# Feed-forward transposes by a trip through HBM and 32x32 block turns on VectorE, in place of TensorE transposes

## The chip, the cores and the metric

One core of a Trainium2 chip. The core has TensorE (PE in the rows; PEld is its weight load), VectorE (DVE), ScalarE (ACT), GpSimd (POOL) and SyncE (SP), each with its own instruction stream, and 16 DMA engines that all queues share. DMAs are issued here by SP and by ACT, each in the order of its own stream. The metric is the device time of one execution in microseconds, median of the runs.

## The reference

One layer of a hybrid decoder trunk, 256 tokens by 2048 features, all in float32. Four token mixers run on one normalised input, their gated sum goes through `w_out`, and a feed-forward part with a short convolution over time follows. The change touches only that last part:

```python
h2 = rmsnorm(x, norm2_g)
u = causal_dwconv(h2 @ ffn_up, ffn_dw, ffn_db)   # 3 taps over time, per feature
a, v = jnp.split(u, 2, axis=-1)                  # 5632 features each
return x + (jax.nn.silu(a) * v) @ ffn_down
```

## The kernel before

**Products.** Every large product (`product`, L192) has 256 tokens, in two halves of 128 rows of PSUM, by 512 output features. The weights stream in from HBM: SP loads 1 MB (four slices of 128 input features by 512) into one of three `wr` buffers (L180). A *unit* is two of those slices. ACT copies a unit into a float32r tile `wh` (L187), DVE computes the rest `wl = wr - wh` (L189), and PE multiplies both with the stationary activations: eight matmuls with `wh` (L205 and L206), then four with `wl` (L211). `wh` and `wl` have three buffers each. At the end of each unit `step` (L148) takes one piece of waiting work from the list `later`.

**Feed-forward.** The 11264 features of `ffn_up` are done in 22 *halves* of 512: for each of 11 *pairs* one half of `a` and one of `v`. A half is one product of 8 units. `half` (L897) then moves the two accumulators to SBUF with the row scale (`pu`, L901, ACT). The product leaves tokens on the partitions, while the convolution and the next product want features there. So `conv` has PE transpose eight 128x128 blocks against the identity into PSUM (`pt`, L908). Each of the four feature blocks then gets its first tap and bias on ACT (L912), two shifted taps on DVE (L916) and, for `a`, the silu on ACT (L921). This is put on `later` and runs two units into the next product. `glu` (L933 and `split_out`) multiplies `a` and `v` and splits the result into `ah` and `al`, the stationary operand of the down product.

**Down products.** `DOWN = (3, 3, 2, 3)` says how many pairs one `down` call (L940) takes. A call runs four products (one per 512 output features) of two units a pair, and adds each to `x2` on DVE (L948). A group's `down` is issued after the first pair of the next group; the last group's also stores the result (L950, SP). Partition p of an activation tile's block j holds feature 128 j + p, and the rows of `ffn_down` are loaded in that order.

**Order.** The program is straight-line code. The tile framework orders each engine's stream from dependencies and code order; the copies of the next units stand ahead of the evacuation `pu` in ACT's stream, as far as the three `wh` buffers go.

Of the kernel before, what the change touches and what calls it, by code (L numbers as in the profile page):

```python
# [9 lines left out]
F32 = mybir.dt.float32  # L10
F32R = mybir.dt.float32r
U8 = mybir.dt.uint8
AF = mybir.ActivationFunctionType
ALU = mybir.AluOpType
# [3 lines left out]
P = 128  # L18
S = 256
NT = 2  # L20
D = 2048
KT = D // P
BW = 512
NB = 4
DFF = 5632
NPAIR = DFF // BW
# [11 lines left out]
NEG = -1e30  # L38
LOAD = 4 * BW
WR = 3  # L40
DOWN = (3, 3, 2, 3)
WINDOWS = (2, 4, 8, 16)


# [54 lines left out]
def layer(ctx, tc, a):  # L99
    nc = tc.nc  # L100
    V, A, T = nc.vector, nc.scalar, nc.tensor
# [4 lines left out]
    ffn_up = a["ffn_up"][0]  # L106
# [3 lines left out]
    ident = cst.tile([P, P], F32, name="ident")  # L110
# [11 lines left out]
    tpp = ctx.enter_context(tc.tile_pool(name="tpp", bufs=2, space=PSUM))  # L122
# [13 lines left out]
    def pump(ns):  # L136
        credit[0] += ns
        while bg and credit[0] > 0:
            try:
                credit[0] -= next(bg[0])  # L140
            except StopIteration:
                bg.pop(0)
        if not bg:
            credit[0] = 0.0

    later = []

    def step(ns):  # L148
        if later:
            f = later.pop(0)  # L150
            if f is not None:
                f()
        else:
            pump(ns)
# [13 lines left out]
    def wtile(name, dt, ks, n, size, bufs=None):  # L168
        w = wp.tile([P, size], dt, name=name, bufs=bufs)
        return w[:, : ks * BW].rearrange("p (j n) -> p j n", j=ks)[:, :, :n]  # L170

    def units(src, c0, n, sizes, loads):

        k0 = have = 0
        loads = list(loads)
        for ks in sizes:
            if k0 == have:
                m = loads.pop(0)
                raw = wtile("wr", F32, m, n, LOAD, WR)
                nc.sync.dma_start(  # L180
                    out=raw,
                    in_=src[k0 * P : (k0 + m) * P, c0 : c0 + n].rearrange("(j p) n -> p j n", p=P),
                )
                base, have = k0, k0 + m
            part = raw[:, k0 - base : k0 - base + ks]
            hi = wtile("wh", F32R, ks, n, 2 * BW)
            A.copy(out=hi, in_=part)  # L187
            lo = wtile("wl", F32R, ks, n, 2 * BW)
            V.tensor_tensor(out=lo, in0=part, in1=hi.bitcast(F32), op=ALU.subtract)  # L189
            yield k0, hi, lo  # L190
            k0 += ks

    def product(src, c0, n, stat, sizes=None, loads=None, tail=False):

        nk = len(stat)
        acc = [accp.tile([P, 512], F32, name="acc") for _ in range(NT)]
        for k0, hi, lo in units(src, c0, n, sizes or [2] * (nk // 2), loads or [4] * (nk // 4)):
            ks = hi.shape[1]
            for ts in ((0,), (1,)) if tail and k0 + ks == nk else ((0, 1),):
                for j in range(ks):  # L200
                    xh, xl = stat[k0 + j]
                    for t in ts:
                        s = slice(t * P, (t + 1) * P)
                        o = acc[t][:, :n]
                        T.matmul(o, xh[:, s], hi[:, j], start=(k0 + j == 0), stop=False)  # L205
                        T.matmul(o, xl[:, s], hi[:, j], start=False, stop=False)  # L206
                for j in range(ks):
                    xh, _ = stat[k0 + j]
                    for t in ts:
                        s = slice(t * P, (t + 1) * P)  # L210
                        T.matmul(  # L211
                            acc[t][:, :n], xh[:, s], lo[:, j], start=False, stop=(k0 + j == nk - 1)
                        )
            step(1200.0)
        return acc

    def rsqrt(pool, ssq, n, scale, tag):

        v = pool.tile([P, n], F32, name=tag + "v", tag=tag + "v")
        V.tensor_scalar(v, ssq, scale, EPS, ALU.mult, ALU.add)  # L220
        r = pool.tile([P, n], F32, name=tag + "r", tag=tag + "r")
        A.activation(r, v, AF.Sqrt)
        V.reciprocal(out=r, in_=r)
        e = pool.tile([P, n], F32, name=tag + "e", tag=tag + "e")
        V.tensor_tensor(out=e, in0=v, in1=r, op=ALU.mult)
        V.tensor_tensor(out=e, in0=e, in1=r, op=ALU.mult)
        V.tensor_scalar(e, e, -0.5, 1.5, ALU.mult, ALU.add)
        V.tensor_tensor(out=r, in0=r, in1=e, op=ALU.mult)
        return r
# [36 lines left out]
    with ExitStack() as ph1:  # L266
# [46 lines left out]
        def vec(name, i=0):  # L313
            return vecT[:, VEC[name] + i : VEC[name] + i + 1]
# [438 lines left out]
        with tc.tile_pool(name="pDB", bufs=1) as pp:  # L753
# [7 lines left out]
            acc = product(w_in, C_CZ + BW, BW, hS, sizes=(1, 1) + (2,) * 7, loads=(1, 1) + (2,) * 7)  # L761
# [13 lines left out]
            for t in range(NT):  # L775
                V.scalar_tensor_tensor(
                    out=sg[:, t], in0=acca[t], scalar=rstd[:, t : t + 1], in1=sg[:, t],
                    op0=ALU.mult, op1=ALU.mult,
# [6 lines left out]
            pw = pp.tile([P, 4, P], F32, name="pw")  # L785
# [47 lines left out]
        with tc.tile_pool(name="pA", bufs=1) as pp:  # L833
            za = pp.tile([P, NT, W_FOX], F32, name="za")
            fb = pp.tile([P, 8], F32, name="fb")
# [30 lines left out]
    h2S = []  # L866
    ss2 = p2.tile([P, NT, 4], F32, name="ss2")
    for d in range(4):
        acc = product(w_out, d * BW, BW, yS)
# [3 lines left out]
        hi = hp.tile([P, 4, S], F32R, name="h2h", tag="h2h")  # L873
        lo = hp.tile([P, 4, S], F32R, name="h2l", tag="h2l")
        for b in range(2):
            pt = tpp.tile([P, 2, S], F32, name="pt")
            for i in range(2):
                c = 4 * d + 2 * b + i
                for t in range(NT):
                    T.transpose(pt[:, i, t * P : (t + 1) * P], x2[:, t, c * P : (c + 1) * P], ident)  # L880
            for i in range(2):
                c = 4 * d + 2 * b + i
# [9 lines left out]
    rstd2 = rsqrt(p2, s2, NT, 1.0 / D, "x2")  # L892


    up_ = ctx.enter_context(tc.tile_pool(name="fu", bufs=2))

    def half(pair, is_v, u):  # L897
        acc = product(ffn_up, (NPAIR if is_v else 0) * BW + pair * BW, BW, h2S)
        pu = up_.tile([P, NT, BW], F32, name="pu")
        for t in range(NT):  # L900
            A.activation(pu[:, t], acc[t], AF.Identity, scale=rstd2[:, t : t + 1])  # L901

        def conv(b):
            pt = tpp.tile([P, 2, S], F32, name="pt")
            for i in range(2):
                c = 2 * b + i
                for t in range(NT):
                    T.transpose(pt[:, i, t * P : (t + 1) * P], pu[:, t, c * P : (c + 1) * P], ident)  # L908
            for i in range(2):
                c = 2 * b + i  # L910
                ch = (NPAIR if is_v else 0) * 4 + pair * 4 + c
                A.activation(  # L912
                    u[:, c], pt[:, i], AF.Identity, bias=vec("fb", ch), scale=vec("fw", 2 * 88 + ch)
                )
                for sh, tap in ((1, 1), (2, 0)):
                    V.scalar_tensor_tensor(  # L916
                        out=u[:, c, sh:], in0=pt[:, i, : S - sh], scalar=vec("fw", tap * 88 + ch),
                        in1=u[:, c, sh:], op0=ALU.mult, op1=ALU.add,
                    )
                if not is_v:  # L920
                    A.activation(u[:, c], u[:, c], AF.Silu)  # L921

        later.extend([None, lambda: (conv(0), conv(1))])

    def pair_up(pair):
        ua = up_.tile([P, 4, S], F32, name="ua")
        uv = up_.tile([P, 4, S], F32, name="uv")
        hi, lo = act_tiles()
        half(pair, False, ua)
        half(pair, True, uv)  # L930

        def glu():
            V.tensor_tensor(out=uv, in0=ua, in1=uv, op=ALU.mult)  # L933
            split_out(hi, lo, uv)

        later.append(glu)
        return hi, lo

    out = a["out"][0].rearrange("(t p) d -> p t d", p=P)

    def down(pairs, tiles, last):
        st = stationary(tiles)
        w = ffn_down[pairs[0] * BW : (pairs[-1] + 1) * BW]
        for d in range(4):
            ds = slice(d * BW, (d + 1) * BW)
            acc = product(w, d * BW, BW, st, tail=last and d == 3)
            for t in range(NT):
                V.tensor_tensor(out=x2[:, t, ds], in0=acc[t], in1=x2[:, t, ds], op=ALU.add)  # L948
                if last:
                    nc.sync.dma_start(out=out[:, t, ds], in_=x2[:, t, ds])  # L950

    pending = None
    p0 = 0
    for size in DOWN:
        pairs = list(range(p0, p0 + size))
# [10 lines left out]
def feature_columns(inputs):  # L966

    cols = [inputs[n][0].reshape(-1, P) for n in ("norm2_g", "pool_scale", "gla_og", "conv_ln_g", "conv_ln_b", "conv_db")]
    cols += [np.tile(inputs[n][0], 2)[None] for n in ("fox_qg", "fox_kg")]
    cols += [inputs[n][0].reshape(-1, P) for n in ("conv_dw", "ffn_dw", "ffn_db")]  # L970
    return np.ascontiguousarray(np.concatenate(cols, axis=0).T)


# [26 lines left out]
```

## Time and profile before

| | |
|---|---|
| median of 3 runs (lowest to highest) | 1529.78 us (1529.42 to 1529.83) |
| the profiled execution's own time | 1529.93 us |
| its span, first to last instruction | 1528.1 us |
| PE busy | 1522.4 us, 100% of the span |
| DVE, ACT busy | 952.2 us (62%), 769.9 us (50%) |
| moved over HBM | 291.12 MB, mean 191 GB/s |
| chain that ended last | PE 99%, DMA 1% |

The chain that ended last is followed back from the last instruction: at every step to what released it. Busy time of PE overlaps (matmuls are pipelined), so the pitch of matmuls, start to start, tells more than the duration of one.

### The profile page before, as it was taken

To read this page: it belongs to the slowest core of one execution; us is meant where nothing else is said; L and a number is where in the kernel's file an instruction comes from. 1 tells how busy PE (TensorE), PEld (TensorE's weight loads), DVE (VectorE), ACT (ScalarE), POOL (GpSimd) and SP (SyncE) were. 2 spreads that over 40 slices of the span, in tenths; PEclk is the share of its full clock that TensorE was granted. 3 is DMA by queue.
4 is the path that set the end of the run, shared out by engine and by line. 5 is a ranking of instruction groups with operands and counts; after the bars stand their busy time and mean duration, and the time that the engine had idled before them with its cause. 6 is when DMAs were issued, how large, how long until landed. Compare 5 with 4: busy or idle time off the path is not lost.

```text
span 1528.1 us, 18387 instructions
## 1 busy us (share of the span) xinstructions
PE 1522.4 (100%) x7196; PEld 1278.0 (84%) x7196; DVE 952.2 (62%) x1220; ACT 769.9 (50%) x961; POOL 0.2 (0%) x4
## 2 busy tenths in 40 slices
PE   9999999999999999999999999999999999999998
PEld 8888899878998888888888888888888888888887
DVE  7799755657565566566555566655566546655664
ACT  6444466545455544444455555434555345535542
POOL 0000000000000000000000000000000000000000
PEclk9999999999999999999999999999999999999999
DMA  9656656545664566657555555555555555565563
GB/s 295 225 188 205 200 178 212 173 151 179 184 214 144 164 203 203 196 172 248 185 175 191 193 179 179 193 193 187 199 179 180 194 193 191 173 206 184 182 206 124
DMA packets 150665, 291.12 MB, mean 191 GB/s; under 512 B 5665, under 2 KB 20914, under 8 KB 150194
## 3 DMA queue, kind: packets, MB, share of 16 engines
q1 hardware_dynamic: 149680, 288.22, 57.4%
q10 hardware_dynamic: 898, 1.74, 0.4%
q8 instruction: 56, 0.92, 0.2%
q14 instruction: 31, 0.25, 0.1%
HBM read 287.83 MB, written 2.10 MB: 190 GB/s over the span
## 4 chain that ended last, share of the span: by engine, by line
PE 99%; DMA 1%; ACT 0%; issue 0%; DVE 0%; ACTq 0%
PE acc L205 32%; PE acc L206 31%; PE acc L211 31%; PE pt L908 1%; PE mx L547 1%; PE mx L739 0%; DMA wr<-in_w_in 0%; PE mx L698 0%; PE pt L880 0%; PE pt L255 0%; DMA n1g<-in_n1T 0%; ACT wh L187 0%; PE mx L731 0%; PE pt L338 0%; PE mx L515 0%
## 5 line engine op out<-in xcount | busy, mean ns | idle before, releaser
L189 DVE TENSOR_TENSOR wl<-wr,wh 128x1024 fp32r<-128x1024 f32 (+4 forms) x545 | 646.9, 1191 | 474.4 <-ACT wh L187 469.8
L187 ACT CAST wh<-wr 128x1024 fp32r<-128x1024 f32 (+4 forms) x545 | 558.9, 1026 | 673.1 <-PE acc L206 603.2
L205 PE MATMUL acc<-wh,ah 128*128 128x512 f32 (+3 forms) x1344 | 515.0, 383 | 0.5 <-ACT wh L187 0.5
L206 PE MATMUL acc<-wh,al 128*128 128x512 f32 (+3 forms) x1344 | 512.0, 381 | 0.0
L211 PE MATMUL acc<-wl,ah 128*128 128x512 f32 (+3 forms) x1344 | 347.4, 380 | 0.0
L205 PEld LDWEIGHTS acc<-wh,ah 128*128 128x128 f32 x1344 | 252.8, 188 | 45.9 <-ACT wh L187 2.1
L206 PEld LDWEIGHTS acc<-wh,al 128*128 128x128 f32 x1344 | 252.8, 188 | 42.8 <-issue 0.6
L211 PEld LDWEIGHTS acc<-wl,ah 128*128 128x128 f32 x1344 | 249.1, 188 | 43.9
L205 PE MATMUL acc<-wh,h2h 128*128 128x512 f32 x704 | 275.7, 392 | 0.0
L206 PE MATMUL acc<-wh,h2l 128*128 128x512 f32 x704 | 274.2, 389 | 0.0
L211 PE MATMUL acc<-wl,h2h 128*128 128x512 f32 x704 | 188.2, 389 | 0.0
L211 PEld LDWEIGHTS acc<-wl,h2h 128*128 128x128 f32 x704 | 132.1, 188 | 27.5
L205 PEld LDWEIGHTS acc<-wh,h2h 128*128 128x128 f32 x704 | 132.2, 188 | 27.0
L206 PEld LDWEIGHTS acc<-wh,h2l 128*128 128x128 f32 x704 | 132.2, 188 | 26.8
L428 DVE SCALAR_TENSOR_TENSOR cacc<-up,vecT,cacc 128x256 f32<-128x256 f32 x120 | 51.0, 484 | 0.0
L205 PE MATMUL acc<-wh,oh 128*128 128x512 f32 x128 | 49.8, 389 | 0.0
L206 PE MATMUL acc<-wh,ol 128*128 128x512 f32 x128 | 49.8, 389 | 0.0
L916 DVE SCALAR_TENSOR_TENSOR ua<-pt,vecT,ua 128x255 f32<-128x255 f32 (+1 forms) x88 | 38.3, 477 | 8.8 <-ACT ua L912 8.0
L916 DVE SCALAR_TENSOR_TENSOR uv<-pt,vecT,uv 128x255 f32<-128x255 f32 (+1 forms) x88 | 37.0, 476 | 2.7 <-ACT uv L912 2.7
L211 PE MATMUL acc<-wl,oh 128*128 128x512 f32 x128 | 35.7, 393 | 0.0
L948 DVE TENSOR_TENSOR x<-acc,x 128x512 f32<-128x512 f32 x32 | 20.7, 686 | 20.7 <-PE acc L211 20.7
L356 DVE SCALAR_TENSOR_TENSOR gt<-acc,rstd,gb 128x512 f32<-128x512 f32 x32 | 22.6, 748 | 13.7 <-PE acc L211 13.7
(229 smaller groups left out, 645.4 us busy)
## 6 DMA issues: line engine op xcount, KB each, us to landing
wr<-in_ffn_up SPq DMA_DIRECT2D x88, 1024.0 KB, 4.9
wr<-in_w_in SPq DMA_DIRECT2D x76, 1024.0 KB, 5.1
wr<-in_ffn_down SPq DMA_DIRECT2D x44, 1024.0 KB, 5.0
wr<-in_w_branch SPq DMA_DIRECT2D x16, 1024.0 KB, 5.0
wr<-in_w_out SPq DMA_DIRECT2D x16, 1024.0 KB, 4.9
wr<-in_w_in SPq DMA_DIRECT2D x16, 772.0 KB, 4.5
wr<-in_w_in SPq DMA_DIRECT2D x8, 696.0 KB, 4.2
gb<-in_gate_b SPq DMA_DIRECT2D x16, 256.0 KB, 3.4
```

The lines of the kernel that those rows point to most:

```text
L187: A.copy(out=hi, in_=part)
L189: V.tensor_tensor(out=lo, in0=part, in1=hi.bitcast(F32), op=ALU.subtract)
L205: T.matmul(o, xh[:, s], hi[:, j], start=(k0 + j == 0), stop=False)
L206: T.matmul(o, xl[:, s], hi[:, j], start=False, stop=False)
L211: T.matmul(acc[t][:, :n], xh[:, s], lo[:, j], start=False, stop=(k0 + j == nk - 1))
L356: V.scalar_tensor_tensor(out=g[:, t], in0=acc[t], scalar=rstd[:, t : t + 1], in1=bias, op0=ALU.mult, op1=ALU.add,)
L428: V.scalar_tensor_tensor(out=acc[:, c], in0=up[:, c, j : j + S], scalar=vec("cw", 4 * j + c), in1=acc[:, c], op0=ALU.mult, op1=ALU.add,)
L547: T.matmul(pss[h][:, q * P : (q + 1) * P], l_, r_, start=True, stop=True)
L908: T.transpose(pt[:, i, t * P : (t + 1) * P], pu[:, t, c * P : (c + 1) * P], ident)
L916: V.scalar_tensor_tensor(out=u[:, c, sh:], in0=pt[:, i, : S - sh], scalar=vec("fw", tap * 88 + ch), in1=u[:, c, sh:], op0=ALU.mult, op1=AL ...
L948: V.tensor_tensor(out=x2[:, t, ds], in0=acc[t], in1=x2[:, t, ds], op=ALU.add)
```

## The change

The eight PE transposes of a half go. In their place `half` does four things.

- ACT writes `pu` with its four feature quarters (128 features each) outermost, and stores quarter q with one DMA into rows 32 q to 32 q + 31 of a scratch tensor `mem` in HBM (128 KB a DMA, in runs of 1 KB). The four token quarters (32 partitions each) become blocks along a row of `mem`. Token quarters and feature quarters have changed places.
- `fetch`: ACT loads `mem` back as `pw` (512 KB, one 4 KB row a partition).
- `turn`: two DVE transposes turn the 32x32 blocks of `pw` into `zt`, features on partitions. Partition p of block j now holds feature 4 p + j of the half, so the columns of `ffn_dw` and `ffn_db` are reordered on their way in, and the rows of `ffn_down` are loaded as `(p j)`.
- `conv(c)`: taps, bias and silu as before, for one block at a time, reading `zt` in SBUF where it was `pt` in PSUM.

These pieces no longer go through `later`. `after(n, engine, f)` sets one due n units on, and ties its instructions behind the latest `wh` copy (ACT) or `wl` subtraction (DVE) of that unit: fetch at 6, turn at 9, the four convolutions at 10 to 13, `glu` at 14. `DOWN` becomes `(3, 3, 2, 2, 1)`: the last `down` takes one pair and follows the `down` of two pairs.

```diff
@@ -38,7 +38,7 @@
 NEG = -1e30
 LOAD = 4 * BW
 WR = 3
-DOWN = (3, 3, 2, 3)
+DOWN = (3, 3, 2, 2, 1)
 WINDOWS = (2, 4, 8, 16)
 
 
@@ -145,7 +145,20 @@
 
     later = []
 
+    due = []
+    steps = [0]
+    mark = {}
+
+    def after(n, engine, f):
+
+        due.append((steps[0] + n, engine, f))
+
     def step(ns):
+        steps[0] += 1
+        for x in [x for x in due if x[0] <= steps[0]]:
+            due.remove(x)
+            with tc.issue_after(mark[x[1]].ins):
+                x[2]()
         if later:
             f = later.pop(0)
             if f is not None:
@@ -169,7 +182,7 @@
         w = wp.tile([P, size], dt, name=name, bufs=bufs)
         return w[:, : ks * BW].rearrange("p (j n) -> p j n", j=ks)[:, :, :n]
 
-    def units(src, c0, n, sizes, loads):
+    def units(src, c0, n, sizes, loads, rows):
 
         k0 = have = 0
         loads = list(loads)
@@ -179,22 +192,22 @@
                 raw = wtile("wr", F32, m, n, LOAD, WR)
                 nc.sync.dma_start(
                     out=raw,
-                    in_=src[k0 * P : (k0 + m) * P, c0 : c0 + n].rearrange("(j p) n -> p j n", p=P),
+                    in_=src[k0 * P : (k0 + m) * P, c0 : c0 + n].rearrange(rows, p=P),
                 )
                 base, have = k0, k0 + m
             part = raw[:, k0 - base : k0 - base + ks]
             hi = wtile("wh", F32R, ks, n, 2 * BW)
-            A.copy(out=hi, in_=part)
+            mark["A"] = A.copy(out=hi, in_=part)
             lo = wtile("wl", F32R, ks, n, 2 * BW)
-            V.tensor_tensor(out=lo, in0=part, in1=hi.bitcast(F32), op=ALU.subtract)
+            mark["V"] = V.tensor_tensor(out=lo, in0=part, in1=hi.bitcast(F32), op=ALU.subtract)
             yield k0, hi, lo
             k0 += ks
 
-    def product(src, c0, n, stat, sizes=None, loads=None, tail=False):
+    def product(src, c0, n, stat, sizes=None, loads=None, tail=False, rows="(j p) n -> p j n"):
 
         nk = len(stat)
         acc = [accp.tile([P, 512], F32, name="acc") for _ in range(NT)]
-        for k0, hi, lo in units(src, c0, n, sizes or [2] * (nk // 2), loads or [4] * (nk // 4)):
+        for k0, hi, lo in units(src, c0, n, sizes or [2] * (nk // 2), loads or [4] * (nk // 4), rows):
             ks = hi.shape[1]
             for ts in ((0,), (1,)) if tail and k0 + ks == nk else ((0, 1),):
                 for j in range(ks):
@@ -893,34 +906,56 @@
 
 
     up_ = ctx.enter_context(tc.tile_pool(name="fu", bufs=2))
+    scr = ctx.enter_context(tc.tile_pool(name="scr", bufs=2, space=bass.MemoryType.DRAM))
 
     def half(pair, is_v, u):
-        acc = product(ffn_up, (NPAIR if is_v else 0) * BW + pair * BW, BW, h2S)
-        pu = up_.tile([P, NT, BW], F32, name="pu")
+
+        n = (NPAIR if is_v else 0) + pair
+        acc = product(ffn_up, n * BW, BW, h2S)
+
+        pu = up_.tile([P, 4, NT, P], F32, name="pu")
         for t in range(NT):
-            A.activation(pu[:, t], acc[t], AF.Identity, scale=rstd2[:, t : t + 1])
-
-        def conv(b):
-            pt = tpp.tile([P, 2, S], F32, name="pt")
-            for i in range(2):
-                c = 2 * b + i
-                for t in range(NT):
-                    T.transpose(pt[:, i, t * P : (t + 1) * P], pu[:, t, c * P : (c + 1) * P], ident)
-            for i in range(2):
-                c = 2 * b + i
-                ch = (NPAIR if is_v else 0) * 4 + pair * 4 + c
-                A.activation(
-                    u[:, c], pt[:, i], AF.Identity, bias=vec("fb", ch), scale=vec("fw", 2 * 88 + ch)
-                )
-                for sh, tap in ((1, 1), (2, 0)):
-                    V.scalar_tensor_tensor(
-                        out=u[:, c, sh:], in0=pt[:, i, : S - sh], scalar=vec("fw", tap * 88 + ch),
-                        in1=u[:, c, sh:], op0=ALU.mult, op1=ALU.add,
-                    )
-                if not is_v:
-                    A.activation(u[:, c], u[:, c], AF.Silu)
-
-        later.extend([None, lambda: (conv(0), conv(1))])
+            A.activation(
+                pu[:, :, t], acc[t].rearrange("p (q x) -> p q x", q=4), AF.Identity, scale=rstd2[:, t : t + 1]
+            )
+
+        mem = scr.tile([P, 4 * NT * P], F32, name="mem")
+        for q in range(4):
+            A.dma_start(
+                out=mem[32 * q : 32 * q + 32].rearrange("r (k c) -> k r c", k=4),
+                in_=pu[:, q].rearrange("p t x -> p (t x)"),
+            )
+        pw = up_.tile([P, 4, NT, P], F32, name="pw")
+
+        def fetch():
+            A.dma_start(out=pw.rearrange("p k t x -> p (k t x)"), in_=mem)
+
+        zt = up_.tile([P, 4, S], F32, name="zt", bufs=1)
+
+        def turn():
+            for t in range(NT):
+                V.transpose(
+                    out=zt[:, :, t * P : (t + 1) * P].rearrange("p j (k i) -> p j k i", k=4),
+                    in_=pw[:, :, t].rearrange("p k (i j) -> p j k i", j=4),
+                )
+
+        def conv(c):
+            ch = n * 4 + c
+            A.activation(
+                u[:, c], zt[:, c], AF.Identity, bias=vec("fb", ch), scale=vec("fw", 2 * 88 + ch)
+            )
+            for sh, tap in ((1, 1), (2, 0)):
+                V.scalar_tensor_tensor(
+                    out=u[:, c, sh:], in0=zt[:, c, : S - sh], scalar=vec("fw", tap * 88 + ch),
+                    in1=u[:, c, sh:], op0=ALU.mult, op1=ALU.add,
+                )
+            if not is_v:
+                A.activation(u[:, c], u[:, c], AF.Silu)
+
+        after(6, "A", fetch)
+        after(9, "V", turn)
+        for c in range(4):
+            after(10 + c, "V", lambda c=c: conv(c))
 
     def pair_up(pair):
         ua = up_.tile([P, 4, S], F32, name="ua")
@@ -933,7 +968,7 @@
             V.tensor_tensor(out=uv, in0=ua, in1=uv, op=ALU.mult)
             split_out(hi, lo, uv)
 
-        later.append(glu)
+        after(14, "V", glu)
         return hi, lo
 
     out = a["out"][0].rearrange("(t p) d -> p t d", p=P)
@@ -943,7 +978,7 @@
         w = ffn_down[pairs[0] * BW : (pairs[-1] + 1) * BW]
         for d in range(4):
             ds = slice(d * BW, (d + 1) * BW)
-            acc = product(w, d * BW, BW, st, tail=last and d == 3)
+            acc = product(w, d * BW, BW, st, tail=last and d == 3, rows="(p j) n -> p j n")
             for t in range(NT):
                 V.tensor_tensor(out=x2[:, t, ds], in0=acc[t], in1=x2[:, t, ds], op=ALU.add)
                 if last:
@@ -967,7 +1002,8 @@
 
     cols = [inputs[n][0].reshape(-1, P) for n in ("norm2_g", "pool_scale", "gla_og", "conv_ln_g", "conv_ln_b", "conv_db")]
     cols += [np.tile(inputs[n][0], 2)[None] for n in ("fox_qg", "fox_kg")]
-    cols += [inputs[n][0].reshape(-1, P) for n in ("conv_dw", "ffn_dw", "ffn_db")]
+    cols += [inputs["conv_dw"][0].reshape(-1, P)]
+    cols += [inputs[n][0].reshape(-1, P, 4).transpose(0, 2, 1).reshape(-1, P) for n in ("ffn_dw", "ffn_db")]
     return np.ascontiguousarray(np.concatenate(cols, axis=0).T)
 
 
```

**ACT's stream, around one `v` half and the `a` half behind it, before.** `wh` is the weight copy, `pu` the evacuation of a half, `uv`/`ua` the first tap, `ah` the split of the pair's result:

```order
L901 ACTIVATE pu<-acc,x2r 128x512 x2
L187 CAST wh<-wr 128x1024 x2
L912 ACTIVATE uv<-pt,vecT 128x256 x4
L187 CAST wh<-wr 128x1024 x2
L234 CAST ah<-uv 128x1024
L187 CAST wh<-wr 128x1024 x4
L901 ACTIVATE pu<-acc,x2r 128x512 x2
```

**The same place after the change:**

```order
L918 ACTIVATE pu<-acc,x2r 128x4x128 x2
L924 DMA mem<-pu 4x32x256 x4
L200 CAST wh<-wr 128x1024 x3
L931 DMA pw<-mem 128x1024
L200 CAST wh<-wr 128x1024
L247 CAST ah<-uv 128x1024
L200 CAST wh<-wr 128x1024 x3
L944 ACTIVATE ua<-zt,vecT 128x256 x4
L200 CAST wh<-wr 128x1024
L918 ACTIVATE pu<-acc,x2r 128x4x128 x2
L953 ACTIVATE ua<-ua 128x256
```

Five DMAs a half now stand in ACT's stream; the fetch stands behind three weight copies, and the first taps of a half now stand after four more copies, one copy ahead of the next half's evacuation.

**DVE's stream, around the end of one pair, before.** `wl` is the weight subtraction:

```order
L189 TENSOR_TENSOR wl<-wr,wh 128x1024 x8
L916 SCALAR_TENSOR_TENSOR uv<-pt,vecT,uv 128x255 x2
L916 SCALAR_TENSOR_TENSOR uv<-pt,vecT,uv 128x254 x2
L916 SCALAR_TENSOR_TENSOR uv<-pt,vecT,uv 128x255 x2
L916 SCALAR_TENSOR_TENSOR uv<-pt,vecT,uv 128x254 x2
L189 TENSOR_TENSOR wl<-wr,wh 128x1024
L933 TENSOR_TENSOR uv<-ua,uv 128x1024
L189 TENSOR_TENSOR wl<-wr,wh 128x1024
L235 TENSOR_TENSOR al<-uv,ah 128x1024
```

**The same half after it:**

```order
L937 STREAM_TRANSPOSE zt<-pw 128x4x128 x2
L202 TENSOR_TENSOR wl<-wr,wh 128x1024
L948 SCALAR_TENSOR_TENSOR uv<-zt,vecT,uv 128x255
L948 SCALAR_TENSOR_TENSOR uv<-zt,vecT,uv 128x254
L202 TENSOR_TENSOR wl<-wr,wh 128x1024
L948 SCALAR_TENSOR_TENSOR uv<-zt,vecT,uv 128x255
L948 SCALAR_TENSOR_TENSOR uv<-zt,vecT,uv 128x254
L202 TENSOR_TENSOR wl<-wr,wh 128x1024
L948 SCALAR_TENSOR_TENSOR uv<-zt,vecT,uv 128x255
L202 TENSOR_TENSOR wl<-wr,wh 128x1024
L948 SCALAR_TENSOR_TENSOR uv<-zt,vecT,uv 128x254
```

The taps, eight in a row before, are spread between the weight subtractions, and two block turns stand ahead of them.

## Rows read from the trace of the kernel before

**Rows 1.** The page, busy time of PE (share of span, instructions).

```profile
PE 1522.4 (100%) x7196; PEld 1278.0 (84%) x7196; DVE 952.2 (62%) x1220; ACT 769.9 (50%) x961; POOL 0.2 (0%) x4
```

**Rows 2.** Chain of waits, one half: start us, length us, engine, tile, line.

```profile
834.37 0.91 PE acc L211 x4
835.28 0.87 PE pt L908 x8
...
854.32 0.91 PE acc L211 x4
857.04 0.91 PE acc L211 x4
```

**Rows 3.** Groups by line: count, busy us, mean ns, idle before.

```profile
L908 PE MATMUL pt<-ident,pu 128*128 128x128 f32 x176 | 22.8, 272 | 0.0
```

**Rows 4.** Waits from 800 us to the end: us in total, times, longest.

```profile
ACT wh L187 <- PE acc L206: 287.5, 191, 1.7
...
PEld acc L205 <- ACT wh L187: 0.7, 1, 0.7
```

**Rows 5.** Busy time in one half: stretch, PE, PEld, DVE, ACT, POOL, clock, DMA share, GB/s.

```profile
834.37:857.04 22.67, 22.67 (x106) 18.85 (x105) 15.18 (x18) 12.47 (x15) 0.00 (x0) 1.00 0.56 186
```

**Rows 6.** Timeline of ACT behind one evacuation: start, length, idle before.

```profile
829.93 1.26 ACT L901 ACTIVATE pu<-acc,x2r 128x512 f32<-128x512 f32 x2
831.69 1.06 ACT L187 CAST wh<-wr 128x1024 fp32r<-128x1024 f32 x1 [0.50 <-PE acc L206]
834.41 1.05 ACT L187 CAST wh<-wr 128x1024 fp32r<-128x1024 f32 x1 [1.66 <-PE acc L206]
```

**Rows 7.** DMA issues by line on ACT's and SP's sequencers: ns min/median/max.

```profile
L806 ACTq DMA_DIRECT2D gx<-in_consts x1: 335/335/335, 202.0 to 202.0; - x1
L813 ACTq DMA_DIRECT2D wab<-in_gla_ba x1: 532/532/532, 202.8 to 202.8; - x1
L180 SPq DMA_DIRECT2D wr<-in_ffn_down x44: 367/368/390, 947.4 to 1501.1; - x44
```

**Rows 8.** DMA queues (packets, MB, share of 16 engines); issues (KB, us to landing).

```profile
q1 hardware_dynamic: 149680, 288.22, 57.4%
q10 hardware_dynamic: 898, 1.74, 0.4%
...
wr<-in_ffn_down SPq DMA_DIRECT2D x44, 1024.0 KB, 5.0
...
out<-x SPq DMA_DIRECT2D x8, 256.0 KB, 2.4
...
sst<-in_consts ACTq DMA_DIRECT2D x1, 512.0 KB, 5.1
...
wab<-in_gla_ba ACTq DMA_DIRECT2D x1, 1.0 KB
```

**Rows 9.** Groups by line from 800 us on, or of the whole run (last row).

```profile
L187 ACT CAST wh<-wr 128x1024 fp32r<-128x1024 f32 x256 | 269.7, 1054 | 313.9 <-PE acc L206 287.5 <-issue 16.4 <-ACT wh L187 10.0
...
L901 ACT ACTIVATE pu<-acc,x2r 128x512 f32<-128x512 f32 x44 | 27.8, 682 | 0.0
L912 ACT ACTIVATE ua<-pt,vecT 128x256 f32<-128x256 f32 x44 | 23.4, 557 | 3.3 <-PE pt L908 3.3
...
L948 DVE TENSOR_TENSOR x<-acc,x 128x512 f32<-128x512 f32 x32 | 20.7, 686 | 20.7 <-PE acc L211 20.7
...
L921 ACT ACTIVATE ua<-ua 128x256 f32<-128x256 f32 x44 | 18.2, 415 | 12.1 <-DVE ua L916 12.1
...
L307 DVE TENSOR_REDUCE sqx<-sqs 128x256 f32<-128x1024 f32 x1 | 2.0, 2003 | 0.0
```

**Rows 10.** Chain of waits at the start of the last down product.

```profile
1465.41 0.91 PE acc L211 x4
...
1476.92 0.91 PE acc L211 x4
```

**Rows 11.** Waits of SP's queue: us in total, times, longest.

```profile
SPq L180 <- DVE wl L189: 1170.7, 240, 9.6
```

## The prediction

> **What bounds the kernel now.** I read the busy times first. PE is busy for the whole span [rows 1], so whatever leaves PE can shorten the run, if nothing else becomes late. The chain of waits says which work on PE that is: in the feed-forward stretch it runs through the matmuls of lines 205, 206 and 211 with the transposes of line 908 between them [rows 2]. The waits of that stretch show the other engines waiting for PE: ACT's weight copies wait 287.5 us for a matmul to free a `wh` buffer, PE waits 0.7 us for a copy, and no wait for a DMA is listed [rows 4]. SP waits 4.9 us on average (1170.7 / 240) for a `wr` buffer before it may issue a load [rows 11]: the loads are early too. In one half of 22.67 us DVE has 15.18 us of work, ACT 12.47 us, and the DMA engines are busy 0.56 of the time; TensorE's clock is at 1.00 of full speed, its upper level [rows 5]. So this stretch is bound by PE's work alone, with slack everywhere else.
>
> **What the change removes.** Two last matmul groups one half apart start at 834.37 and 857.04 us, 22.67 us; two neighbouring units start at 854.32 and 857.04, 2.72 us [rows 2]. Eight units are 21.76 us, so the eight transposes take 0.91 us of the chain (the chain's own piece is 0.87). The busy time of line 908 (22.8 us over 176 transposes [rows 3]) counts overlapped ends; the pitch is the better price. 176 / 8 = 22 halves, 22 x 0.91 = **20.0 us** less on PE. A second, small term: at the start of the last `down`, units that should stand 4 x 2.72 = 10.88 us apart stand 1476.92 - 1465.41 = 11.51 us apart [rows 10], since the last pair's taps crowd ACT and DVE while PE already needs its product. With one pair in the last group, the two-pair `down` (16 units) lies between, so these **0.6 us** go.
>
> **What it adds, and what hides it.**
>
> *DMA issues on ACT.* Issues on ACT's sequencer took 0.34 to 0.53 us [rows 7]; I take 0.53 for each write, since the nearest in kind is unclear: 4 x 0.53 + 0.45 = 2.6 us a half, on top of ACT's 12.47 of what will be 21.76. Behind the four writes stand three weight copies. The first of them is due 0.50 us after the evacuation [rows 6], so it comes about 1.6 us late (plus a silu of 0.42 [rows 9] in every other half). A copy has room: three buffers let it start 0.91 + 2 x 2.72 = 6.35 us before its matmuls, and it takes 1.05 [rows 9], so 5.3 us may pass before PE waits. Cost nothing. Without that cover it would be 22 x 2.6 = 57 us.
>
> *The trip to HBM.* ACT reaches the fetch behind three copies, the last of which starts no earlier than 831.69 + 2 x 2.72 = 837.13 and ends at 838.2, that is 6.9 us after the first write could be issued at 831.3 ([rows 6], put in the new order). The fetch waits for all four writes, and behind it in ACT's stream queue the weight copies, for which DVE and then PE wait. So the landing of the writes matters. The nearest row is the store of the output, 256 KB in 2.4 us [rows 8]. What a DMA engine needs for a byte follows from the first queue: 0.574 x 1528.1 x 16 / 288.22 MB is 0.050 us for 1 KB. Spread over 16 engines, a half's 512 KB is 1.6 us an engine; the store's share is 0.8 of its 2.4, so 1.6 us are fixed. With an idle engine the writes land 3.2 us after the first issue, with only the 0.44 that the loads leave free [rows 5] 5.2 us. Both are below 6.9. The far end, all on fewer engines, is the first rival.
> How late may they land? Once ACT is held at the fetch, one turn of its stream is: fetch issue 0.45, four copies 4.2, four first taps at some 0.51 each 2.0, one copy 1.05, two evacuations 1.26, silus 0.6 on average [rows 6, 7, 9], 9.6 us in all until the next first write. 21.76 - 9.6 = 12.1 us; DVE's turn, for which the first taps wait, may take about 1 us of that. So from a landing at **11 to 12 us** on, every further microsecond costs one in each half, 22 us in the run. I take 5 us: no cost.
>
> *The fetch itself* (512 KB) has the constants' 512 KB at 5.1 us beside it [rows 8]. Four copies, 10.9 us, stand between it and the first taps. Hidden, from the store's 2.4 to twice the 5.1.
>
> *The block turns* are not in this trace. A VectorE operation over 128x512 from the accumulators took 0.686 us; a reduction that reads 1024 elements with a stride took 2.0 [rows 9]. Two turns a half are 1.4 to 4.0 us, on DVE's 15.18, against 21.76: 16.6 to 19.2. I take 0.7 each, since the inner runs are whole blocks. Cost nothing.
> [...]
>
> *With one answer:* first taps and shifted taps read SBUF instead of PSUM, the evacuation writes with a stride, `glu` comes later, and there are 8 more additions to `x2` of 0.69 us (a fifth `down`): all on ACT and DVE beside PE's work. The `(p j)` loads of `ffn_down` keep 2 KB runs and 1 MB, 5.0 us [rows 8] and 0.37 us to issue [rows 7]; at either end of [rows 7], 0.34 or 0.53, SP's 4.9 us of waiting hides the issue. PE's matmuls, their number and the tail (last addition, last store) stay.
>
> **The sum.** 1529.93 (the profiled execution) - 20.0 - 0.6 + 0 = **1509.3 us**; that execution lies 0.15 us above the median, so I say 1509. Its own range is 1506 to 1513.
>
> **Rivals.**
>
> *1. The writes land too late (slower).* Each write goes out as 4 blocks of 32 rows on the HBM side. If the DMA hardware shares it out by that outermost count, only 4 of 16 engines carry it, the same four for all 88 writes. Then an engine has 128 KB a half: 6.4 us alone, 6.4 / 0.44 = 14.5 us in the gaps of the loads, landing 8.0 to 16.1 us after the first issue. The trace hints at such a rule: of the second queue's 898 packets [rows 8], 785 are data of ACT's eight loads (six of 128 rows, one of 16, one of 1), which leaves 113 = 7 x 16 + 1. The one-row load was closed by one engine, not 16, and shows no landing time. At 14 us, 2 past the limit: 22 x 2 = 44 us, **1553 us**; at 16.1 about 1597; it decides from about 12 us and turns the gain into a loss from 13 us (20.6 / 22 = 0.94 further). For it: the packet count. Against it: at the near end, 8 to 11 us, even four engines cost PE nothing, since ACT may stand still for 5 us.
> [...]
>
> *2. DVE becomes the bound.* At twice the strided reduction's time a turn is 4.0 us, 8 a half; 23.2 us against 21.76, 22 x 1.4 = 31 us, 1541 us. Against it: 1024 strided elements took 2.0 us, a turn has 512.
>
> *3. Not all is given back.* ACT's copies, now in bursts, reach PE late by some tenths: 0.3 us a half gives 1516, 0.91 gives 1529, no change. Against it: 5.3 us of room.
>
> **How the numbers follow.** Hidden as forecast 0.60 (four engines near the fast end included). Rival 1 0.27, spread from 1515 upwards: still faster 0.06, even 0.05, slower 0.16. Rival 2 0.05: slower 0.04, faster 0.01. Rival 3 0.08: faster 0.07, even 0.01. A measurement here tells 0.2%, 3.1 us. Faster 0.74, within 0.06, slower 0.20. The range goes from 1506 to rival 1's 1553, which leaves out its far end, some 0.13.
>
> **What would show it.** Right: no PE piece between two halves, halves of 21.76 us; the writes landing 3 to 11 us after issue; ACT's copies still waiting for PE; turns near 0.7 us; DVE near 75% of a half. Wrong: PE waiting for `wh` copies once a half, with ACT standing at the fetch for a write's landing of 12 us or more (rival 1), or DVE without idle time (rival 2).

## The result, and the profile after

The changed kernel takes 1508.96 us (median of 4 runs, 1508.69 to 1509.41) beside 1529.80 us for the kernel before: a ratio of 0.9864 [0.9847, 0.9882], 20.84 us faster. The profiled execution took 1508.69 us, with a span of 1506.9 us and a granted clock of 1.00. The forecast was 1509 us.

PE is still the bound. The page's busy line of the kernel after (it answers to [rows 1]):

```profile
PE 1501.5 (100%) x7020; PEld 1259.6 (84%) x7020; DVE 997.9 (66%) x1272; ACT 768.6 (51%) x961; POOL 0.2 (0%) x4
```

176 instructions have left PE, and DVE has 45.7 us more to do (952.2 before). The chain of waits after, first over one half and then at the start of the last `down` (start us, length us, engine, tile, line; L224 is the old L211):

```profile
832.96 0.91 PE acc L224 x4
...
854.72 0.91 PE acc L224 x4
...
1464.00 0.91 PE acc L224 x4
...
1466.72 0.91 PE acc L224 x4
...
1472.16 0.91 PE acc L224 x4
```

A half now takes 854.72 - 832.96 = 21.76 us, against 22.67 in [rows 2], and no `pt` piece stands in the chain. At the last `down` the pitch is an even 2.72 us, where [rows 10] had 0.6 us too much.

Busy time in two neighbouring halves after (stretch, total and then PE, PEld, DVE, ACT, POOL, granted clock, DMA share, GB/s), against [rows 5]:

```profile
834.37:856.13 21.76, 21.76 (x97) 18.02 (x96) 15.13 (x19) 12.42 (x18) 0.00 (x0) 1.00 0.70 242
857.00:878.76 21.76, 21.76 (x97) 18.02 (x97) 16.80 (x21) 12.85 (x17) 0.00 (x0) 1.00 0.72 241
```

DVE is at 70 to 77% of a half, and the DMA engines went from 0.56 to 0.70 and more. PE has no idle time in either half.

The waits from 800 us to the end (us in total, times, longest; L200 is the `wh` copy, L953 the silu, L944 the first tap), to set beside [rows 4]:

```profile
ACT wh L200 <- PE acc L219: 233.8, 159, 2.3
...
ACT wh L200 <- DMA mem<-pu: 9.3, 4, 2.4
...
ACT uv L944 <- DVE zt L937: 8.2, 11, 1.4
ACT ua L944 <- DVE zt L937: 6.8, 11, 0.9
ACT ua L953 <- DMA mem<-pu: 6.8, 3, 2.3
```

ACT still waits for PE far more than for anything else. What is new: it waits for the writes of `mem`, which it did not do by the forecast. No wait of PE stands in that stretch's list, so nothing of it reaches PE. One half on ACT's timeline after (start, length, instruction, idle time before it; ACTq is ACT's sequencer, L924 the four writes, L931 the fetch), against [rows 6]:

```profile
851.20 1.25 ACT L918 ACTIVATE pu<-acc,x2r 128x512 f32<-128x512 f32 x2
852.48 2.23 ACTq L924 DMA_DIRECT2D mem<-pu  x4
854.75 2.00 ACT L200 CAST wh<-wr 128x1024 fp32r<-128x1024 f32 x2 [2.31 <-PE acc L219]
857.48 1.06 ACT L200 CAST wh<-wr 128x1024 fp32r<-128x1024 f32 x1 [0.73 <-PE acc L219]
861.14 0.33 ACTq L931 DMA_DIRECT2D pw<-mem  x1
861.60 1.05 ACT L200 CAST wh<-wr 128x1024 fp32r<-128x1024 f32 x1 [3.06 <-PE acc L224]
```

The third copy starts at 857.48. In `a_16` (below) the fetch goes out 0.1 us behind the start of that copy, so here ACT could have issued it near 857.6, some 5.1 us after the first write was issued. It issues it after 861.14 - 852.48 = 8.7 us. The 3.06 us of idle time before the last row are put down to PE, but in them ACT's sequencer stood at the fetch and waited for the writes. Over the 22 halves the fetch comes 8.2 us (7.8 to 8.8) after the first write's issue; the last packet of the writes is seen 7.8 us after it.

The block turns, from the groups of the page (busy us, mean ns, idle before):

```profile
L937 DVE STREAM_TRANSPOSE zt<-pw 128x512 f32<-128x512 f32 x44 | 45.7, 1079 | 0.0
```

and the issues of DMAs (ns min/median/max), against [rows 7]:

```profile
L924 ACTq DMA_DIRECT2D mem<-pu x88: 521/538/617, 808.0 to 1441.7; - x88
L931 ACTq DMA_DIRECT2D pw<-mem x22: 321/327/399, 816.4 to 1448.6; - x22
L193 SPq DMA_DIRECT2D wr<-in_ffn_down x44: 539/540/652, 944.1 to 1480.0; - x44
```

A turn takes 1.08 us. Four writes and the fetch take ACT 4 x 0.538 + 0.327 = 2.5 us a half. The `(p j)` loads of `ffn_down` take 0.54 us to issue instead of 0.37, under SP's waiting time.

### The profile page after: what moved, and what is told of

Its sections match the earlier page's. It is cut to its first block, busy times and chain, and to the rows that moved or that the text cites. A ratio compares the mean times of both kernels' runs of the same rounds, so it can differ in the third digit from the quotient of the medians.

```text
span 1506.9 us, 18227 instructions
## 1 busy us (share of the span) xinstructions
PE 1501.5 (100%) x7020; PEld 1259.6 (84%) x7020; DVE 997.9 (66%) x1272; ACT 768.6 (51%) x961; POOL 0.2 (0%) x4
## 2 busy tenths in 40 slices
DMA packets 165450, 314.19 MB, mean 209 GB/s; under 512 B 6369, under 2 KB 32882, under 8 KB 164978
## 4 chain that ended last, share of the span: by engine, by line
PE 99%; DMA 0%; DVE 0%; issue 0%; ACT 0%; ACTq 0%
PE acc L218 32%; PE acc L219 32%; PE acc L224 32%; PE mx L560 1%; DMA wr<-in_w_in 0%; PE mx L752 0%; PE mx L130 0%; PE mx L711 0%; PE pt L893 0%; PE pt L268 0%; PE mx L744 0%; PE pt L351 0%; PE mx L528 0%; PE mx L584 0%; PE mx L613 0%; PE mx L527 0%
## 5 line engine op out<-in xcount | busy, mean ns | idle before, releaser
L200 ACT CAST wh<-wr 128x1024 fp32r<-128x1024 f32 (+4 forms) x545 | 555.7, 1024 | 628.4 <-PE acc L219 548.7
L224 PE MATMUL acc<-wl,ah 128*128 128x512 f32 (+3 forms) x1344 | 347.3, 380 | 0.0
L224 PEld LDWEIGHTS acc<-wl,ah 128*128 128x128 f32 x1344 | 249.1, 188 | 43.8
L224 PE MATMUL acc<-wl,h2h 128*128 128x512 f32 x704 | 188.2, 389 | 0.0
L224 PEld LDWEIGHTS acc<-wl,h2h 128*128 128x128 f32 x704 | 132.1, 188 | 27.4
L937 DVE STREAM_TRANSPOSE zt<-pw 128x512 f32<-128x512 f32 x44 | 45.7, 1079 | 0.0
L953 ACT ACTIVATE ua<-ua 128x256 f32<-128x256 f32 x44 | 18.2, 414 | 48.8 <-issue 20.8
L948 DVE SCALAR_TENSOR_TENSOR uv<-zt,vecT,uv 128x255 f32<-128x255 f32 x88 | 41.7, 481 | 1.3
L948 DVE SCALAR_TENSOR_TENSOR ua<-zt,vecT,ua 128x255 f32<-128x255 f32 x88 | 41.3, 480 | 0.8
L983 DVE TENSOR_TENSOR x<-acc,x 128x512 f32<-128x512 f32 x40 | 25.8, 685 | 15.6 <-PE acc L224 15.6
```

Source lines behind the costliest of these rows:

```text
L200: mark["A"] = A.copy(out=hi, in_=part)
L224: T.matmul(acc[t][:, :n], xh[:, s], lo[:, j], start=False, stop=(k0 + j == nk - 1))
L937: V.transpose(out=zt[:, :, t * P : (t + 1) * P].rearrange("p j (k i) -> p j k i", k=4), in_=pw[:, :, t].rearrange("p k (i j) -> p j k i", ...
L948: V.scalar_tensor_tensor(out=u[:, c, sh:], in0=zt[:, c, : S - sh], scalar=vec("fw", tap * 88 + ch), in1=u[:, c, sh:], op0=ALU.mult, op1=AL ...
```

## The experiments

The trace after shows PE with 20.9 us less of work, gone at the places forecast. Three things remained to be tested: whether the eight transposes cost what the pitch says; whether the writes really run on four engines (the first rival's ground); and how far the kernel is from the point where the landing costs time. `b_twice`, `a_16`, `a_w8` and `a_w8_16` have a kernel before of 1530.11 us beside them, the others one of 1529.48 us. `b_` marks an edit of the kernel before, `a_` one of the kernel after. Times to the fetch run from the first write's issue to the fetch's, as the mean over the 22 halves. Where ACT stands at the fetch this is the landing of the writes; where it doesn't, the writes landed earlier, so the end of their last packet is given too.

### b_twice: every feed-forward transpose of the kernel before twice

```diff
-                for t in range(NT):
+                for t in (0, 1, 0, 1):
```

> The kernel before with every feed-forward transpose done twice (the second writes the same block again). Theory (eight transposes cost PE 0.91 us of pitch, and all of it is on the path): 22 x 0.91 = 20.0 us slower than before, 1550 us. Rival (part of a transpose is hidden beside the matmuls, or its price is the 272 ns of one instruction): 0 to 10, or 22 x 8 x 0.272 = 48 us slower.

1549.41 us (1548.77 to 1549.93), ratio 1.0127 [1.0112, 1.0142]: 19.3 us more, the span 19.8 us more. One piece of its chain of waits:

```profile
836.76 1.75 PE pt L908 x16
```

Sixteen transposes take twice the 0.87 us of eight [rows 2]: 22 x (1.75 - 0.87) = 19.4 us. So the price of the removed work is confirmed by adding it once more (0.88 us a half added, 0.91 taken out), and neither a price of 272 ns for each transpose nor a part hidden beside the matmuls fits.

### b_down: the kernel before with the new `DOWN` alone

```diff
-DOWN = (3, 3, 2, 3)
+DOWN = (3, 3, 2, 2, 1)
```

> The kernel before with the down products split as (3, 3, 2, 2, 1) alone. Theory: the 0.6 us that PE loses at the start of the last down product goes and nothing else changes, 1529.2 us, which the trace shows and the time does not. Rival (a fifth down call with its 8 additions and 2 MB of stores nearer the end costs at the tail): 1 to 5 us slower.

1528.62 us (1528.15 to 1530.19, 10 runs), ratio 0.9996 [0.9986, 1.0005]. The time does not tell this edit from nothing; the chain of waits does:

```profile
1464.54 0.91 PE acc L211 x4
...
1475.41 0.91 PE acc L211 x4
```

Four units take 10.87 us, the even pitch, where [rows 10] have 11.51. The 0.6 us are real in the trace, and belong to this line alone.

### a_16: the same writes, cut by token quarter instead of feature quarter

```diff
-        for q in range(4):
+        for k in range(4):
             A.dma_start(
-                out=mem[32 * q : 32 * q + 32].rearrange("r (k c) -> k r c", k=4),
-                in_=pu[:, q].rearrange("p t x -> p (t x)"),
+                out=mem.rearrange("(q r) (k c) -> k r q c", q=4, k=4)[k],
+                in_=pu[32 * k : 32 * k + 32].rearrange("p q t x -> p q (t x)"),
```

> The changed kernel with each of the four writes of a half cut by token quarter (32 partitions by 4 feature quarters) in place of feature quarter: same bytes, same 1 KB runs, but 32 is now the outermost count on both sides. Theory (a write is shared out by its outermost count; the four-engine writes land about 8 us after the first issue, which ACT's room of 11 to 12 us hides): the writes run on 16 engines, land 3 to 5.5 us after the first issue, ACT no longer stands at the fetch, and the time stays at 1509 us (1507 to 1511). Rival (ACT's standing at the fetch, 16 us in all, reaches PE): some microseconds faster, down to 1493. Rival (the number of engines does not depend on the shape): landing stays at 8 us.

1508.67 us (1508.03 to 1509.45), ratio 0.9859 [0.9843, 0.9876]: the time of the kernel after. The second queue on the pages of the kernel after and of `a_16` (packets, MB, share):

```profile
q10 hardware_dynamic: 15682, 24.81, 4.7%
```

```profile
q10 hardware_dynamic: 16738, 24.81, 4.8%
```

The kernel before had 898 packets on it [rows 8]. Of the 14784 new ones after, 88 x 128 are runs of 1 KB and 22 x 128 rows of 4 KB, which leaves 704 = 88 x 4 + 22 x 16. They are small packets: the two pages count 5665 and 6369 of under 512 B, 704 more. Read as one such packet from each engine that took part, a write is closed by 4 engines, a fetch by 16 (`a_w8` rules out other sums). With the other cut the remainder is 1760 = 88 x 16 + 22 x 16. So read, the same bytes in the same runs went over 4 or 16 engines by shape alone. ACT's timeline of `a_16`:

```profile
853.26 3.07 ACTq L924 DMA_DIRECT2D mem<-pu  x4
856.37 2.96 ACT L200 CAST wh<-wr 128x1024 fp32r<-128x1024 f32 x3 [3.14 <-PE acc L219]
858.41 0.34 ACTq L931 DMA_DIRECT2D pw<-mem  x1
```

The fetch is issued 5.6 us (5.1 to 6.1) after the first write, as soon as ACT gets to it, and no wait for `mem` is left. The fetch comes 2.6 us earlier (the writes' last packet ends after 4.0 us instead of 7.8) and the time is the same: at 8.2 us the four engines are hidden.

### a_w8 and a_w8_16: all four writes twice, on 4 and on 16 engines

The second set goes to another scratch tensor that nobody reads, and is issued ahead of the first. `a_w8_16` has the cut of `a_16` for both sets.

```diff
+        mem2 = scr.tile([P, 4 * NT * P], F32, name="mem2")
+        for q in range(4):
+            A.dma_start(
+                out=mem2[32 * q : 32 * q + 32].rearrange("r (k c) -> k r c", k=4),
+                in_=pu[:, q].rearrange("p t x -> p (t x)"),
+            )
```

> The changed kernel with every write issued twice on ACT, first into a second scratch tensor that nothing reads. Theory: still four engines, now with 256 KB each a half; the last write lands some 15 us after the first issue, 3 to 4 us beyond the limit of 11 to 12; PE waits for weight copies in every half, 22 x 3.5 = 77 us, 1586 us (1550 to 1620). Rival (ACT's and the copies' room is larger than worked out, or the landing is not what holds ACT): 1509 to 1515.

> Every write issued twice as well, but cut by token quarter. The same number of issues, bytes and runs as the kernel with doubled writes by feature quarter. Theory (it is the four engines that make the landing late, not the issues or the bytes): the last write lands 6 to 9 us after the first issue, and the time stays near 1509 us (1507 to 1513). Rival (issue time on ACT, 8 x 0.54 = 4.3 us a half, or the bytes in HBM cost the time): as slow as its partner, above 1540.

| | time, us | ratio to before | to the fetch, us | last packet, us |
|---|---|---|---|---|
| `a_w8` | 1620.20 (1617.85 to 1622.77) | 1.059 [1.0574, 1.0606] | 14.2 (13.5 to 15.6) | 13.8 |
| `a_w8_16` | 1517.44 (1516.55 to 1518.98) | 0.9919 [0.9904, 0.9934] | 6.2 (5.8 to 6.9) | 5.7 |

The two differ in the shape of the writes alone, and in 103 us. The second queue of `a_w8`:

```profile
q10 hardware_dynamic: 27298, 36.34, 6.5%
```

Beyond the 898 of the kernel before and the data (176 x 128 and 22 x 128) this leaves 1056 = 176 x 4 + 22 x 16. Together with the 704 of the kernel after, only 4 for a write and 16 for a fetch fit that reading.

The waits of `a_w8` from 790 us on:

```profile
...
PEld acc L218 <- ACT wh L200: 90.9, 25, 6.9
ACT ua L959 <- DMA mem<-pu: 90.6, 17, 7.0
...
ACT wh L200 <- DMA mem<-pu: 53.1, 9, 7.0
```

These are the signs that the prediction gave for its first rival: ACT stands for the landing, and PE for a copy, once a half. But it isn't the copies behind the fetch that PE waits for. ACT's timeline of one half (L925 and L930 are the two sets of writes, L937 the fetch):

```profile
862.28 2.23 ACTq L925 DMA_DIRECT2D mem<-pu  x4
864.55 4.70 ACTq L930 DMA_DIRECT2D mem<-pu  x4
869.28 2.94 ACT L200 CAST wh<-wr 128x1024 fp32r<-128x1024 f32 x3 [7.04 <-issue]
876.55 0.33 ACTq L937 DMA_DIRECT2D pw<-mem  x1
876.98 2.00 ACT L200 CAST wh<-wr 128x1024 fp32r<-128x1024 f32 x2 [4.75 <-DMA mem<-pu]
```

PE stands still from 868.2 to 870.4, until the first copy behind the eight writes is done, and not at the copies behind the fetch. So it is with each of its 22 stops of more than 1 us. The landing lengthens ACT's turn (14.2 us to the fetch and 12.8 from there to the next first write, 27.0 us instead of 21.76), and the place where PE feels it is the issue of the writes, 6.9 us here against 4.2 us in `a_w8_16`. `a_w8` alone can't part the two; `a_w8_late` (below) does so in part.

It is 34 us slower than expected. The limit is lower than forecast (`a_w6`, below), and after some of its long stops PE runs at a granted clock near 0.50. Four neighbouring stretches of `a_w8` (columns as above):

```profile
884.00:892.00 8.00, 8.00 (x37) 6.64 (x36) 5.94 (x8) 4.48 (x8) 0.00 (x0) 1.00 0.66 232
892.00:898.50 6.50, 0.43 (x2) 0.01 (x1) 0.00 (x0) 1.37 (x3) 0.00 (x0) 0.84 0.27 88
898.50:903.00 4.50, 4.46 (x11) 3.50 (x12) 4.48 (x6) 1.88 (x2) 0.00 (x0) 0.50 0.62 183
903.00:911.00 8.00, 8.00 (x36) 6.63 (x35) 4.57 (x6) 3.67 (x5) 0.00 (x0) 0.98 0.89 319
```

PE stands still from 892 to 898.5. Then the granted clock is 0.50, half of the first row's 1.00, for 4.5 us, in which 11 matmuls run instead of some 20. From 790 us on 97 matmuls have a pitch near 0.43 instead of 0.23 us: about 20 of the 111 us that `a_w8` lies above the kernel after; 88 us are standstill.

`a_w8_16` is 8.5 us above the kernel after, where none were expected, with an earlier fetch. So four more issues and 512 KB more a half cost about that; the remaining 103 us of `a_w8` hang on the four engines, by the landing and the longer issue together.

### a_w6: six writes on four engines

```diff
+        mem2 = scr.tile([P, 4 * NT * P], F32, name="mem2")
+        for q in range(2):
+            A.dma_start(
+                out=mem2[32 * q : 32 * q + 32].rearrange("r (k c) -> k r c", k=4),
+                in_=pu[:, q].rearrange("p t x -> p (t x)"),
+            )
```

> The changed kernel with six writes a half: two of the four are issued once more, ahead, into a second scratch tensor that nothing reads. Four writes landed so that the fetch was issued 8.2 us after the first issue, eight at 14.2 us, so six should come to some 11.2. Doubling cost 111 us, of which PE stood still 88 us (4.0 a half), which puts the limit at 14.2 - 4.0 = 10.2 us. Revised theory: 22 x (11.2 - 10.2) = 22 us slower than the changed kernel, 1531 us (1518 to 1545). By the limit of the prediction, 11 to 12 us: 1509 to 1513 us.

1553.04 us (1552.24 to 1553.90), ratio 1.0155 [1.014, 1.017], 11.7 us (10.9 to 12.9) to the fetch, the last packet after 11.2 us. Both forecasts of the time were too low, that by the prediction's limit of 11 to 12 us by far: at 11.7 us the loss is 44.1 us, 2.0 a half, which, all put down to the landing, sets the limit near 11.7 - 2.0 = 9.7 us. Some 8 of the 44 us are slow matmuls (39 with a pitch near 0.43 us, as at the clock of 0.50 in `a_w8`; the mean granted clock of this run is 0.994); without them it is 10.1 us. Where the forecast of it went wrong is seen on ACT's timeline of `a_w6`:

```profile
869.06 0.33 ACTq L937 DMA_DIRECT2D pw<-mem  x1
869.48 1.05 ACT L200 CAST wh<-wr 128x1024 fp32r<-128x1024 f32 x1 [5.95 <-PE acc L219]
870.43 1.04 ACT L247 CAST ah<-uv 128x1024 fp32r<-128x1024 f32 x1
871.38 2.94 ACT L200 CAST wh<-wr 128x1024 fp32r<-128x1024 f32 x3
877.19 2.08 ACT L950 ACTIVATE ua<-zt,vecT 128x256 f32<-128x256 f32 x4 [2.86 <-DVE zt L943]
879.18 1.04 ACT L200 CAST wh<-wr 128x1024 fp32r<-128x1024 f32 x1
880.12 1.24 ACT L918 ACTIVATE pu<-acc,x2r 128x512 f32<-128x512 f32 x2
...
881.39 1.08 ACTq L925 DMA_DIRECT2D mem<-pu  x2
```

From the fetch to the next first write ACT needs 881.39 - 869.06 = 12.3 us, not 9.6; over the halves with no `down` between it is 12.3 us too (11.4 to 14.1). The sum had four copies, four taps, a copy and the evacuation right, but not the 2.86 us that ACT waits for the turn (it had at most 1), nor the 1.04 us of `glu`'s `ah`, which stands in every other half. 21.76 - 12.3 = 9.4 us is left for the landing, close to the 9.7 to 10.1 from the time.

### a_w8_late: a_w8 with everything behind the writes two units later

```diff
-        after(6, "A", fetch)
-        after(9, "V", turn)
+        after(8, "A", fetch)
+        after(11, "V", turn)
...
-            after(10 + c, "V", lambda c=c: conv(c))
+            after(12 + c, "V", lambda c=c: conv(c))
...
-        after(14, "V", glu)
+        after(16, "V", glu)
```

> The kernel with every write doubled on four engines, and fetch, turn, taps and glu each due two units (5.4 us) later. Theory (doubling cost 111 us because ACT stands at the fetch while weight copies queue behind it): ACT reaches the fetch about when the writes land, the standing goes, and the time comes back to 1509 to 1520 us. Rival (four DMA engines with 256 KB a half slow down the weight loads themselves): it stays above 1580 us.

1571.26 us (1567.44 to 1572.70), ratio 1.027 [1.0253, 1.0287]: between the two. 49 of the 111 us of `a_w8` came back, so the landing was part of them; 62 us stayed. The chain that ended last, by engine, in `a_w8` and in `a_w8_late`:

```profile
PE 74%; ACTq 8%; DMA 6%; ACT 6%; issue 3%; DVE 2%; DVEq 0%
```

```profile
PE 83%; ACTq 10%; ACT 5%; issue 1%; DMA 1%; DVE 0%
```

The DMAs have nearly left the chain, and the issuing on ACT's sequencer (ACTq) has not. ACT's timeline of `a_w8_late` shows it:

```profile
856.82 2.29 ACTq L925 DMA_DIRECT2D mem<-pu  x4
859.13 4.69 ACTq L930 DMA_DIRECT2D mem<-pu  x4
863.92 1.04 ACT L200 CAST wh<-wr 128x1024 fp32r<-128x1024 f32 x1 [7.13 <-PE acc L224]
```

The second four writes take 4.69 us to issue, the first four 2.29. ACT's copy starts 7.1 us after its last work, past the 5.3 us of room. Eight issues span 6.9 us a half in `a_w8` and 7.5 here, but 4.2 in `a_w8_16`: with the writes on four engines the issuing engine is held longer. My theory had counted the wait at the fetch alone and fell short. Late loads aren't the rest: ACT waits 20 us for `wr` in this kernel, but never with the first copy behind the writes, and each of PE's 22 stops of more than 1 us ends with that copy.

### a_turn2: each block turn twice

```diff
-            for t in range(NT):
+            for t in (0, 1, 0, 1):
```

> The changed kernel with each of the two block turns of a half done twice (the second writes the same block again). A turn took 1.08 us where 0.7 was forecast; doubling adds 2.2 us a half to DVE, 15.1 to 16.8 becoming up to 19 of 21.76 us. Theory (DVE has that room): 1509 us (1507 to 1512). Rival (DVE, or the first taps that wait for the turn, is near its limit): 22 x 1 us or more, 1531 us.

1514.18 us (1512.76 to 1514.89), ratio 0.990 [0.9885, 0.9914]: 5.2 us more than the kernel after, where nothing was expected. The waits from 790 us on:

```profile
ACT uv L944 <- DVE zt L937: 38.7, 11, 4.9
ACT ua L944 <- DVE zt L937: 37.4, 11, 5.1
```

Two more turns a half, 2.2 us, make ACT wait 76 us for `zt` instead of 15. DVE is at 69% of the span, far from a bound; the turn lies on the chain fetch, turn, taps, copy, evacuation, writes. PE's gaps add up to 5.8 us, in a few places (1.53 at 923.5 us, 1.48 at 969.2). So the kernel after has room for about 2 us on that chain, and in a few halves less.

## Why the prediction was right, and where its steps were not

**The sum.** 20.0 and 0.6 us were forecast, 20.84 measured between the medians. The half went from 22.67 to 21.76 us, and each of the two terms was shown alone (`b_twice` in the time, `b_down` in the trace only). From the first matmul of `ffn_up` to the last of all, the traces differ by 739.4 - 718.9 = 20.5 us; the first one comes 0.5 us earlier in the kernel after, behind code that the change leaves alone. The pitch was the right price, not the duration of one transpose (272 ns each would be 48 us).

**What hides the rest.** No wait of PE appears, but the margins were not those forecast:

- *Landing: 5 us taken, 8.2 measured to the fetch, 7.8 to the last packet.* The first rival's ground was true by the packet counts: 704 more packets in the kernel after give 4 engines a write, 1760 in `a_16` 16, and against my choice it was 4. Its near end (8.0 us) is what came; the far end, at the loads' idle share, did not. With 4, 6 and 8 writes the last packet ends after 7.8, 11.2 and 13.8 us: if all writes share the same four, that is 128 KB more an engine in 6.0 us, 0.047 us a KB, close to the 0.050 that the prediction took for an engine without other work.
- *Limit: 11 to 12 us taken, 9.4 to 10.1 by `a_w6`.* The sum of ACT's own work was nearly right (it left out `ah`), the wait for DVE's turn inside it was not. And ACT, once late, stopped PE for more than 1 us only with the first copy behind the writes, not with the copies behind the fetch as the prediction had it.
- *Reaching the fetch: 6.9 us taken, 5.6 measured* (`a_16`). ACT stands at the fetch sooner than forecast.
- Together, the forecast margin of 6 us is 1.2 to 1.9 (about 2 by `a_turn2`). The rival failed by no more than that: at 11.7 us (`a_w6`) the gain has turned into a loss, and at 14.2 us (`a_w8`) the time is 90 us above that of the kernel before. The prediction had counted four engines near the fast end as hidden, so its zero stands; that the margin held although both of its sides were mis-sized was luck.
- *Turn: 0.7 us taken, 1.08 measured,* between the bounds, nearer the lower. DVE has room, so the second rival fails; but `a_turn2` shows that it is the turn's latency that counts, not its share of DVE.
- *Issues:* 2.6 us a half forecast, 2.5 measured, hidden. `ffn_down`'s loads rose to the upper of the two rows taken (0.54), hidden as forecast.

The third rival (a few tenths given back each half) did not occur: from 790 us on PE's trace has no gap of more than 0.1 us between matmuls, and the time leaves no room for it.

## What to carry to other kernels

Price what leaves a bound engine by the pitch of its chain before and after. For what is hidden, work out the margin too, with the waits between engines in it: here it was 1.2 to 2 us a half, and 0.94 us past it in each half would have cost the whole gain. Price the issuing too: it is there, and not at the wait, that PE felt the late writes. Look at the blocks that a DMA's two sides are cut into: a layout that reads naturally (four feature quarters, each 128 partitions into four blocks of 32 rows) put each write on 4 engines by its packets, and the same bytes cut the other way (32 partitions into 32 rows of four blocks) on 16, which brought the fetch 2.6 us forward at no cost (1508.67 us beside 1508.96). Two shapes don't show which of these counts decides.

## What the runs showed of the hardware that was not expected

- The issue of a DMA had no fixed price: 0.54 us each for the first four writes, 0.65 to 1.4 for the next four behind them (means of `a_w8`, 4 engines a write by the packets), 6.9 us for the eight. With the cut for sixteen engines the eight took 4.2 us (`a_w8_16`).
- After a standstill of about 6 us PE ran at a granted clock of 0.50 for 4.5 us (`a_w8`, 892 to 903). So a stall of PE cost more than itself in `a_w8`: 20 us on top of 88. It did not take 6 us: in `a_w8_16` a stop of 1.8 us at 968.4 was followed by 0.50 from 971.5 to 974.9, while in `a_w6` one of 1.7 us at 910.5 was not. What decides, these runs don't show.
- A block turn of 128x512 fp32 on DVE took 1.08 us, more than an addition of the same shape (0.69 [rows 9]).
